# Value products' bank as one room, attention rows joined in DRAM during the recurrence, and softmax inverses two rows at a time

## The chip, the cores and the metric

The kernel runs on one core of a Trainium2 chip. The metric is the device time of one execution in microseconds; several executions give a median. A profile of one further execution tells when each engine worked. The engines are TensorE (matrix products; its weight loads are listed apart), VectorE, ScalarE, GpSimd (POOL in the profile) and SyncE (SP), which here only issues transfers. ScalarE and GpSimd issue transfers as well. 16 DMA engines move the data; transfers issued by SP and ScalarE go over hardware queues (q1, q10), those issued by GpSimd over a software queue (q0).

## What is computed

One step of a one-layer streaming encoder on 1024 prompt positions and 64 sample positions, 1088 columns in all, with 1024 channels:

```python
xn = rms_norm(x, g_pre)
z = xn @ w_in
xa, ga, q, k, v, gb, fl, ma, mb = jnp.split(z, ...)
ua, conv_new = causal_conv(xa, conv_hist, conv_w, conv_b)
ya, h_new = rg_lru(ua, h0, w_rg_a, b_rg_a, w_rg_x, b_rg_x, a_param)      # branch A: recurrence
ya = ya * jax.nn.silu(ga)
logf = jax.nn.log_sigmoid(fl + b_f)
yb = fox_attend(...)             # branch B: softmax(q k^T / 8 + cum_q - cum_k, causal) v, 16 heads of 64
yb = yb.reshape(B, L, W_B) * jax.nn.silu(gb)
u = jnp.einsum('bsnw,nwd->bsnd', jnp.stack([ya, yb], axis=2), w_branch)
gates = jax.nn.sigmoid(jnp.stack([ma, mb], axis=2))
mix = jnp.sum(gates * u, axis=2) @ w_o
h = x + rms_norm(mix, g_post)
ple = jax.nn.sigmoid(h @ w_ple_gate) * (pe @ w_ple_proj)
h = h + rms_norm(ple, g_ple)
```

All is float32. The products reach that precision by splitting each operand into a high part (`xh`, `wh`) and the rest (`xl`, `wl`) and adding three products of parts.

## The kernel before

Data lie with channels on the 128 partitions and positions along the row. The program's stages follow each other on TensorE: the input norm and the value projection; the query and key projections and others in a scheme with sums of weight blocks; attention (about 440 to 850 us); the recurrence of branch A (846 to 1010 us), the branch projections, the merge, the output projection and the embedding part.

**Attention.** A head's 1024 prompt queries are taken in four units of 256. For each unit the scores are made in a bank of the accumulating memory (`s`, L1212 and L1213), VectorE adds the mask and finds the row's minimum (`nm`), ScalarE takes the exponential and the row's sum `sm` (L1191). GpSimd takes the sum to the power of -1 against a column of -1 (`warm`, L1193) and multiplies the row by it (L1194). TensorE turns the row over in 128-column blocks (`tp`, L1244), ScalarE and VectorE split it (`th`, `tl`), and TensorE multiplies by the values (`pv`, L1265 and L1267). The values' high and low parts lie side by side, so the product has 128 partitions: the low half (64 to 127) must be added to the high half (0 to 63). ScalarE copies one half out (`lo`), VectorE adds the other to it (`y`, L1293), and GpSimd stores the 64 x 256 result to `d_y` (L1297). `d_y[k]` holds heads 2k and 2k+1, 128 rows of 1088 columns; the last 64 columns are the sample positions'.

The bank for `pv` is 128 x 2 x 256: two units have a half each, and the planner's list `v_free` has two entries. Eight sample pairs go through the same bank.

**The order of the work** in attention is made by a planner when the program is built. `book(engine, ready, cost, emit)` puts an operation behind what that engine has booked so far; constants give the costs in ns (`A_LO` 380 for the copy, `D_Y` 420 for the add, `G_INV` 220 for the power, `HOP` and `HOP_PE` between engines). Where the next attention step isn't due yet, TensorE gets a step of another projection (`acc`, L179 to L181). In the result each engine's order is fixed, and engines wait for each other by semaphores.

**The recurrence.** Eight blocks of 128 channels. Each brings panels of weights, three to a round of the loop that treats two blocks. A panel of 128 x 1024 weights (512 KB) is loaded by SP into `w_raw` (L265); ScalarE copies it to `wh` and copies the negative of `wh` to `wl` (L90); GpSimd issues an accumulating transfer that adds `w_raw` to `wl` (L297, printed `wl<-w_raw`, from the core's own memory to itself). Only then may `w_raw` be filled with the next panel. The convolved block `u` is split by ScalarE (`uh`, behind the panel's copies in ScalarE's order) and VectorE (`ul`) for the gates' products (`gacc`).

**The branch projection** loads block k of `d_y` and of the gate, `d_gb[k]`, in `branch_in` (L1820 and L1821).

Of the kernel before, what the change touches and what calls it, by code (L numbers as in the profile page):

```python
# [8 lines left out]
F32 = mybir.dt.float32  # L9
F32R = mybir.dt.float32r  # L10
AF = mybir.ActivationFunctionType
ALU = mybir.AluOpType
AX = mybir.AxisListType

P = 128
D = 1024
KT = D // P
SEQ = 1024
DEC = 64
T = SEQ + DEC  # L20
# [3 lines left out]
HD = 64  # L24
# [14 lines left out]
GC = 364  # L39

HOP_PE, HOP = 250.0, 90.0
D_MAX, D_LO, D_Y, D_YS = (240.0, 1.035), (130.0, 1.1), 420.0, 230.0
A_EXP, A_HI, A_LO, A_ST, A_W = (450.0, 0.85), (150.0, 0.88), 380.0, 470.0, 1060.0
G_NORM, G_INV = (260.0, 0.84), 220.0
G_DMA = 860.0
D_W = 1240.0

# [26 lines left out]
def hybrid_step(tc, a, o):  # L74
# [14 lines left out]
    def copy_act(out, in_, scale=1.0):  # L89
        return act.activation(out=out, in_=in_, func=AF.Copy, scale=scale)  # L90
# [8 lines left out]
    d_cq = dram.tile([2, NH, DEC], F32, name="d_cq")  # L99
    d_ma = dram.tile([KT, P, T], F32, name="d_ma")  # L100
    d_mb = dram.tile([KT, P, T], F32, name="d_mb")
    d_y = dram.tile([NP, P, T], F32, name="d_y")
    d_gb = dram.tile([KT, P, T], F32, name="d_gb")
    d_ga = dram.tile([KT, P, T], F32, name="d_ga")
    d_x = [dram.tile([P, T], F32, name=f"d_x{k}") for k in range(2)]
# [107 lines left out]
    def chunk(steps):  # L213
        for _ in range(KT):
            next(steps)
# [325 lines left out]
    at = 0  # L541
# [491 lines left out]
    def spent(ns):  # L1033
        now[0] += ns
# [21 lines left out]
    def per(cost, n):  # L1056
        return cost[0] + cost[1] * n
# [117 lines left out]
        at = book("G", smp_at[p], 490.0, lambda: pool.tensor_copy(vs[:, :, 0, :], v_smp[:, :, :]))  # L1175
        t["vs_at"] = book("G", at, 740.0, lambda: sub(pool, vs[:, :, 1, :], v_smp[:, :, :], f(vs[:, :, 0, :])))

    def tiny2(name):
        return p2.tile([P, 1], F32, name=name, tag=name, bufs=12 if name == "nm" else 8)[:, :]

    def lowest(s, w, out, m, least=-NEG):

# [1 line left out]
        return nm, book("D", now[0] + HOP_PE, per(D_MAX, w), lambda: dve.tensor_tensor_reduce(  # L1184
            out=out, in0=s[:, :w], in1=m, scale=-1.0, scalar=least, op0=ALU.add, op1=ALU.min, accum_out=nm))

    def softmax(at, nm, n, pr):


        sm = tiny2("sm")  # L1190
        at = book("A", at, per(A_EXP, n), lambda: act.activation(  # L1191
            out=pr[:, :n], in_=pr[:, :n], func=AF.Exp, scale=-1.0, bias=nm, accum_out=sm))
        at = book("G", at, G_INV, lambda: pool.tensor_tensor(out=sm, in0=sm, in1=warm[:, :], op=ALU.pow))  # L1193
        return book("G", at, per(G_NORM, n), lambda: pool.tensor_scalar(  # L1194
            out=pr[:, :n], in0=pr[:, :n], scalar1=sm, scalar2=1.0, op0=ALU.mult, op1=ALU.mult))

    def width(q2, par):
        n = 256 * q2 + (par + 1) * P
# [4 lines left out]
    def scores(x, i, pr):  # L1203

        h, q2 = units[x]
        t = heads[h]
        half, par = divmod(i, 2)
        n, w = width(q2, par)
        q0 = (2 * q2 + par) * P
        c = slice(half * w, (half + 1) * w)  # L1210
        s = p2s.tile([P, 512], F32, name="s", tag="s")
        pe.matmul(s[:, :w], t["q1"][:, q0:q0 + P], t["k1"][:, c], start=True, stop=False)  # L1212
        pe.matmul(s[:, :w], t["q2"][:HD + 4, q0:q0 + P], t["k2"][:HD + 4, c], start=False, stop=True)  # L1213
        spent(logits_ns(w))
        nm, at = lowest(s, w, pr[:, c], mask[:, SEQ - n + c.start:SEQ - n + c.stop],
                        nm_first.pop((x, par)) if half else -NEG)
        if c.stop < n:
            nm_first[x, par] = nm
            return at, at
        return at, softmax(at, nm, n, pr)  # L1220

    turned, turned_by = {}, {}
    n_diag = [0]
# [27 lines left out]
        return book("D", at, per(D_LO, n), lambda: sub(dve, tl[:, :n], tp[:, :n], f(th[:, :n])))  # L1251

    pvs = {}
    lo_free = [0.0]
    def values(u, g, h, q2):
        vv = heads_v[h]
        if g == 0:
            pvs[u] = pv_half()
        pv = pvs[u]
        th, tl = turned.pop((u, g))  # L1260
        high = turned_by.pop((u, g))
        def part(j, x, **kw):
            v = vv[:, 2 * g + j, :, :].rearrange("p s d -> p (s d)")
            if g < q2:
                return pe.matmul(pv[:, :256], v, x[:, j * 256:(j + 1) * 256], **kw)  # L1265
            c0 = P if j else 0
            return pe.matmul(pv[:, c0:256], v, x[:, :P] if j else x[:, P:3 * P], **kw)  # L1267

        def high_part(j, stop=False):
            tc.declare_no_dep(part(j, th, start=False, stop=stop).ins, high.ins, reason="ordered through the low part")  # L1270

        if g < q2:
            for j in range(2):
                part(j, tl, start=(g == 0 and j == 0), stop=False)
                high_part(j)
            spent(480.0)
            return
        if q2 == 0:
            part(0, tl, start=True, stop=False)
            part(1, tl, start=False, stop=False)  # L1280
            high_part(1)
        else:
            part(1, tl, start=False, stop=False)
            high_part(1)
            part(0, tl, start=False, stop=False)
        high_part(0, True)
        spent(460.0)
        lo = p2.tile([HD, 256], F32, name="lo", tag="lo", bufs=1)
        y = p2.tile([HD, 256], F32, name="y", tag="y", bufs=3)

        dst = d_y[h // 2][(h % 2) * HD:(h % 2 + 1) * HD, q2 * 256:(q2 + 1) * 256]
        at = book("A", max(now[0] + HOP_PE, lo_free[0]), A_LO, lambda: copy_act(lo[:, :], pv[HD:, :256]))
        at = book("D", at, D_Y, lambda: dve.tensor_tensor(out=y[:, :], in0=pv[:HD, :256], in1=lo[:, :], op=ALU.add))  # L1293
        v_free.popleft()
        v_free.append(at)
        lo_free[0] = at
        book("G", at, G_DMA, lambda: pool.dma_start(dst, y[:, :]))  # L1297


# [10 lines left out]
    def sample_scores(p):  # L1310
        t = smp[p]
        s = p2s.tile([P, 512], F32, name="s", tag="s")
        three(s[:, :LS], *(x[:, :] for x in qs + t["ks"]), True, False)
        pe.matmul(s[:, :LS], cs_q[:, :], cs_k[:, :], start=False, stop=True)
        spent(440.0)
        nm, at = lowest(s, LS, prs_s[:, :LS], mask_s[:, :])
        return at, softmax(at, nm, LS, prs_s)

    def sample_turn(p):
        t = smp[p]  # L1320
# [9 lines left out]
    def sample_values(p):  # L1330
        t = smp.pop(p)
        pv = pv_half()
        for i in range(2):
            pe.matmul(pv[:, :], t["vs"][:, i, 0, :], t["pt"][:, i, :, :].rearrange("p s n -> p (s n)"),
                      start=(i == 0), stop=False)
            pe.matmul(pv[:, :P], t["vs"][:, i, 1, :], t["pt"][:, i, 0, :], start=False, stop=(i == 1))
        spent(458.0)
        ys = p2.tile([P, DEC], F32, name="ys", tag="ys", bufs=1)
        ats = []
        for j in range(2):  # L1340
            js, ks = slice(j * HD, (j + 1) * HD), slice(P + j * HD, P + (j + 1) * HD)
            ats.append(book("A", now[0] + HOP_PE, per(A_HI, HD), lambda js=js, ks=ks: copy_act(ys[js, :], pv[js, ks])))
        for j, at in enumerate(ats):
            js = slice(j * HD, (j + 1) * HD)
            at = book("D", at, D_YS, lambda js=js: dve.tensor_tensor(out=ys[js, :], in0=pv[js, js], in1=ys[js, :],
                                                                     op=ALU.add))
        book("D", at, 0.0, lambda: sp.dma_start(d_y[p][:, SEQ:], ys[:, :]))
        v_free.popleft()
        v_free.append(at)

# [19 lines left out]
    due = {}  # L1372
    s_free = deque([0.0, 0.0, 0.0])
    t_free = deque([0.0, 0.0])
    v_free = deque([0.0, 0.0])
    prs = {}
    seen = {"t": 0, "v": 0}
    last_t = {u: ("t", u, q2) for u, (h, q2) in enumerate(units)}
# [62 lines left out]
            t_free.append(due[step])  # L1441
        done.add(step)

    pool.memset(warm[:, :], -1.0)
    booking = tc.manual_schedule(engines={act.engine, dve.engine, pool.engine})
    booking.__enter__()
    load_head(0)
# [238 lines left out]
    class Held:  # L1686
# [8 lines left out]
        def part(self, ks, evac=None, cs=range(len(CH))):  # L1695
            for c in cs:
# [6 lines left out]
                if evac:  # L1703
                    evac(c, t0, n, self.accs[c][:, :n])

    seq = tc.manual_schedule(engines={act.engine, dve.engine})
    seq.__enter__()
    ga = own_gate(0)
# [4 lines left out]
    for k in range(0, KT - 2, 2):  # L1713
        ga = own_gate(k) if k else ga
        if k == 0:
            run(ga)
        gate(k)
        convolve(k + 1)
        mix_u(k)
        if k:  # L1720
            early_gate(k - 1)
        if k:
            split_y(k - 2)
            chunk(ga)
        split_u(k + 1)
        if k:
            chunk(ga)
            state(k - 1)
            output(k - 1)
            run(ga)  # L1730
        own_gate(k + 1)
        xa = recur_in(k + 2)
        chunk(xa)
        chunk(xa)
        if k:
            split_y(k - 1)
        run(xa)
        gate(k + 1)
        convolve(k + 2)
        mix_u(k + 1)  # L1740
        decay(k)
        xa = recur_in(k + 3)
        split_u(k + 2)
        decay_a(k)
        chunk(xa)
        decay(k + 1)
        decay_a(k + 1)
        chunk(xa)
        root(k)
        root(k + 1)  # L1750
        set_sigmoid()
        state(k)
        output(k)
        run(xa)
# [12 lines left out]
    tag, w = panel()  # L1767
    assert tag == ("f", KT - 1)
    fill = panel_steps(mm, *w, xs, lambda c, t0, n, z: spill(d_mb[KT - 1], t0, n, z))
    chunk(fill)  # L1770
    early_gate(k - 1)
    output(k - 1)
# [44 lines left out]
        return ybpool.tile([P, T], dt, name=name, tag=f"yb{i}{k}")  # L1817

    def branch_in(k, t, z):
        sp.dma_start(t[:, :], d_y[k])  # L1820
        sp.dma_start(z[:, :], d_gb[k])  # L1821
        return t, z

# [574 lines left out]
```

## Time and profile before

| | us |
|---|---|
| runs | 1428.65, 1431.42, 1431.19; median 1431.19 |
| profiled execution, its own time | 1429.49 |
| its span | 1427.5 |
| TensorE busy | 1410.8 |
| VectorE, ScalarE, GpSimd busy | 899.4, 720.5, 436.5 |
| TensorE's granted clock, mean | 0.998 of full |

In a row that groups instructions stand line, engine, operation, what is written and from what, the shape of the output and inputs, the count, then busy time in us and mean ns of one, and then the idle time of the engine just before them with what ended most of it. A row of the waits names the engine and line that waited, whom it waited for, and total, number and longest in us. A row of the timeline has start and duration in us, and in brackets the idle time before. A row of a transfer queue has its packets, the MB and the share of the 16 DMA engines' time in that window. A row of transfers' issues has the count, KB of each and us from issue to landing.

### The profile page before, as it was taken

The numbers are of one execution on the slowest core, as the hardware profiler recorded it, in microseconds if no ns is written. First come the engines' busy times: TensorE is split into PE (matmuls) and PEld (weight loads), VectorE is DVE, ScalarE is ACT, GpSimd is POOL, SyncE is SP. The second block draws the span as 40 slices with busy tenths as digits, with TensorE's granted clock in tenths as the row PEclk, the third lists the DMA queues.
The fourth block names the chain that finished last, engine by engine and source line by source line (L and its number), as shares of the span: only waits on it lengthen the run. The fifth ranks groups of instructions, "written<-read, shape, count | busy, mean of one in ns | idle before, by whom it ended". The sixth has DMA issues, their size and how long they took to land.

```text
span 1427.5 us, 25022 instructions
## 1 busy us (share of the span) xinstructions
PE 1410.8 (99%) x9217; PEld 1358.0 (95%) x9217; DVE 899.4 (63%) x1638; ACT 720.5 (50%) x1339; POOL 436.5 (31%) x652
## 2 busy tenths in 40 slices
PE   9999999999999999999999999999999999999997
PEld 8999999999999999999999999999999999888887
DVE  5564766564432666666666656898767474777654
ACT  5423544442222666666666657777544232565443
POOL 0012322233204777768776841221011000000001
PEclk9999999999999999999999999999999999999999
DMA  6667556765247764556566545564467774224211
GB/s 225 214 133 107 150 155 193 162 180 141 85 122 194 182 130 131 137 110 151 123 150 131 84 101 106 83 101 84 165 211 264 252 237 136 113 74 150 78 48 45
DMA packets 138919, 201.20 MB, mean 141 GB/s; under 512 B 24372, under 2 KB 98844, under 8 KB 137772
## 3 DMA queue, kind: packets, MB, share of 16 engines
q1 hardware_dynamic: 119436, 158.96, 44.2%
q0 software_dynamic: 8160, 23.25, 5.9%
q10 hardware_dynamic: 11200, 17.38, 3.4%
q8 instruction: 73, 1.20, 0.3%
q14 instruction: 50, 0.41, 0.1%
HBM read 131.60 MB, written 66.36 MB: 139 GB/s over the span
## 4 chain that ended last, share of the span: by engine, by line
PE 82%; DVE 6%; DMA 5%; ACT 3%; issue 3%; POOL 1%; SPq 0%; DVEq 0%; ACTq 0%; POOLq 0%
PE quad L844 17%; PE acc L179 11%; PE acc L181 11%; PE acc L180 11%; PE q L2042 5%; PE tp L1244 4%; PE pv L1265 3%; PE s L1213 2%; PE s L1212 2%; PE pv L1267 2%; PE vacc L179 1%; PE vacc L180 1%; PE vacc L181 1%; DMA w_raw<-in_w_in 1%; PE vacc L500 1%
## 5 line engine op out<-in xcount | busy, mean ns | idle before, releaser
L179 PE MATMUL acc<-xh,wh 128*128 128x364 f32 x720 | 237.6, 330 | 0.2 <-ACT st L90 0.2
L181 PE MATMUL acc<-xh,wl 128*128 128x364 f32 x720 | 235.8, 328 | 0.0
L180 PE MATMUL acc<-xl,wh 128*128 128x364 f32 x720 | 235.8, 327 | 0.0
L179 PEld LDWEIGHTS acc<-xh,wh 128*128 128x128 f32 x720 | 135.4, 188 | 1.2 <-ACT st L90 0.5
L180 PEld LDWEIGHTS acc<-xl,wh 128*128 128x128 f32 x720 | 135.3, 188 | 0.8
L181 PEld LDWEIGHTS acc<-xh,wl 128*128 128x128 f32 x720 | 135.1, 188 | 0.0
L90 ACT ACTIVATE wh<-w_raw 128x1024 fp32r<-128x1024 f32 (+1 forms) x66 | 63.4, 962 | 86.4 <-PE quad L844 34.4
L93 DVE TENSOR_TENSOR wl<-w_raw,wh 128x1024 fp32r<-128x1024 f32 (+1 forms) x55 | 62.5, 1138 | 67.6 <-ACT wh L90 47.0
L1193 POOL TENSOR_TENSOR sm<-sm,warm 128x1 f32<-128x1 f32 x136 | 79.2, 582 | 57.0 <-ACT pb L1191 21.8
L93 DVE TENSOR_TENSOR tl<-tp,th 128x512 fp32r<-128x512 f32 x96 | 65.6, 687 | 38.7 <-ACT th L90 37.9
L844 PE MATMUL quad<-xh,wh 128*128 128x272 f32 x416 | 87.4, 291 | 1.8 <-ACT p__3330 L90 1.8
L844 PE MATMUL quad<-xl,wh 128*128 128x272 f32 x416 | 86.1, 288 | 0.0
L844 PE MATMUL quad<-xh,wl 128*128 128x272 f32 x416 | 86.0, 288 | 0.0
L1191 ACT ACTIVATE pb<-pb,nm 128x896 f32<-128x896 f32 (+1 forms) x64 | 63.3, 989 | 24.0 <-DVE nm L1184 21.3
L90 ACT ACTIVATE th<-tp 128x512 fp32r<-128x512 f32 x96 | 56.4, 592 | 31.0 <-PE tp L1244 30.3
L2338 POOL TENSOR_TENSOR junk<-ple,g_ple 128x256 f32<-128x256 f32 x4 | 3.8, 956 | 213.2 <-DVE ple L2295 213.2
L1212 PE MATMUL s<-k,q 128*128 128x128 f32 (+2 forms) x192 | 67.5, 353 | 0.0
L844 PEld LDWEIGHTS quad<-xh,wh 128*128 128x128 f32 x416 | 65.3, 188 | 2.3 <-ACT p__3330 L90 2.0
L1213 PE MATMUL s<-k,q 68*128 68x128 f32 (+2 forms) x192 | 65.3, 344 | 0.5 <-issue 0.5
L844 PEld LDWEIGHTS quad<-xh,wl 128*128 128x128 f32 x416 | 65.5, 188 | 0.0
L844 PEld LDWEIGHTS quad<-xl,wh 128*128 128x128 f32 x416 | 65.4, 188 | 0.0
L1194 POOL TENSOR_SCALAR pb<-pb,sm 128x896 f32<-128x896 f32 (+1 forms) x64 | 61.5, 962 | 6.2
(744 smaller groups left out, 4230.4 us busy)
## 6 DMA issues: line engine op xcount, KB each, us to landing
w_raw<-in_w_in SPq DMA_DIRECT2D x56, 256.0 KB
q<-d_q SPq DMA_DIRECT2D x48, 256.0 KB
k<-d_k SPq DMA_DIRECT2D x48, 256.0 KB
w_raw<-in_w_in SPq DMA_DIRECT2D x64, 128.0 KB
w_raw<-in_w_branch SPq DMA_DIRECT2D x32, 256.0 KB
wl<-w_raw POOLq DMA_DIRECT2D x11, 512.0 KB, 4.5
wraw<-in_w_in SPq DMA_DIRECT2D x20, 256.0 KB
d_k<-oh ACTq DMA_DIRECT2D x16, 272.0 KB
```

The lines of the kernel that those rows point to most:

```text
L90: return act.activation(out=out, in_=in_, func=AF.Copy, scale=scale)
L93: return eng.tensor_tensor(out=out, in0=in0, in1=in1, op=ALU.subtract)
L179: pe.matmul(out, ah, bh, start=start, stop=False)
L180: pe.matmul(out, ah, bl, start=False, stop=False)
L181: pe.matmul(out, al, bh, start=False, stop=stop)
L844: pe.matmul(acc[:, c, :CW], l[:, k, :], r[:, k, c * CW:(c + 1) * CW], start=(first and k == 0 and p == 0), stop=(k == 3 and p == 2), skip_ ...
L1191: at = book("A", at, per(A_EXP, n), lambda: act.activation(out=pr[:, :n], in_=pr[:, :n], func=AF.Exp, scale=-1.0, bias=nm, accum_out=sm))
L1193: at = book("G", at, G_INV, lambda: pool.tensor_tensor(out=sm, in0=sm, in1=warm[:, :], op=ALU.pow))
L1194: return book("G", at, per(G_NORM, n), lambda: pool.tensor_scalar(out=pr[:, :n], in0=pr[:, :n], scalar1=sm, scalar2=1.0, op0=ALU.mult, op1 ...
L1212: pe.matmul(s[:, :w], t["q1"][:, q0:q0 + P], t["k1"][:, c], start=True, stop=False)
L1213: pe.matmul(s[:, :w], t["q2"][:HD + 4, q0:q0 + P], t["k2"][:HD + 4, c], start=False, stop=True)
L2042: pe.matmul(acc, l[:, k, :], r[:, k, :], start=(first and k == 0 and i == 0), stop=(k == 3 and i == 2), skip_group_check=not first)
```

## The change

- `d_y` becomes `[8, 2, 128, 1024]`: for each head both halves of the product are stored, and the sample's 64 columns go to a tile of their own, `d_ys`.
- A unit's bank is emptied by one ScalarE copy of 128 x 256 to `y`; GpSimd stores it whole. `v_free` has one entry. For a sample pair there is the same copy, and VectorE adds its halves from there.
- `join_rows(k)` adds, in DRAM, the low halves of block k's two heads to the high halves: one accumulating transfer on GpSimd's queue. Two stand in each round of the recurrence's loop, two behind the recurrence's last panel.
- `branch_in` reads block k in two loads of 64 rows and one of the sample's columns.
- The sums of a unit's two blocks of queries stand in one tile of two columns; VectorE takes both reciprocals in one operation. The planner's cost for it is `INV` 165; the column `warm` is no longer filled for it.

```diff
-    def softmax(at, nm, n, pr):
...
-        at = book("G", at, G_INV, lambda: pool.tensor_tensor(out=sm, in0=sm, in1=warm[:, :], op=ALU.pow))
+    def inverse(at, sm, k):
+        return book("D", at, INV, lambda: dve.reciprocal(out=sm[:, :k], in_=sm[:, :k]))
...
+        if par == 0:
+            sm = tiny2("sm", 2)
+            sums[x] = sm, powers(at, nm, n, pr, sm[:, :1]), pr, n
+            return at, at
+        sm, first, pr0, n0 = sums.pop(x)
+        done_ = inverse(max(first, powers(at, nm, n, pr, sm[:, 1:])), sm, 2)
+        return at, normal(normal(done_, n0, pr0, sm[:, :1]), n, pr, sm[:, 1:])
...
-        lo = p2.tile([HD, 256], F32, name="lo", tag="lo", bufs=1)
-        y = p2.tile([HD, 256], F32, name="y", tag="y", bufs=3)
-        dst = d_y[h // 2][(h % 2) * HD:(h % 2 + 1) * HD, q2 * 256:(q2 + 1) * 256]
-        at = book("A", max(now[0] + HOP_PE, lo_free[0]), A_LO, lambda: copy_act(lo[:, :], pv[HD:, :256]))
-        at = book("D", at, D_Y, lambda: dve.tensor_tensor(out=y[:, :], in0=pv[:HD, :256], in1=lo[:, :], op=ALU.add))
+        y = p2.tile([P, 256], F32, name="y", tag="y", bufs=3)
+        dst = d_y[h // 2, h % 2][:, q2 * 256:(q2 + 1) * 256]
+        at = book("A", now[0] + HOP_PE, A_Y, lambda: copy_act(y[:, :], pv[:, :256]))
         v_free.popleft()
         v_free.append(at)
...
-    v_free = deque([0.0, 0.0])
+    v_free = deque([0.0])
...
+    def join_rows(k):
+        tc.keep_in_program_order(pool.dma_start(d_y[k][:, :HD, :], d_y[k][:, HD:, :],
+                                 accum_op=ALU.add, max_dma_last_dim=4096))
...
         own_gate(k + 1)
         xa = recur_in(k + 2)
+        join_rows(k)
...
         xa = recur_in(k + 3)
+        join_rows(k + 1)
...
     fill = panel_steps(mm, *w, xs, lambda c, t0, n, z: spill(d_mb[KT - 1], t0, n, z))
+    join_rows(k)
+    join_rows(k + 1)
...
     def branch_in(k, t, z):
-        sp.dma_start(t[:, :], d_y[k])
+        for j in range(2):
+            sp.dma_start(t[j * HD:(j + 1) * HD, :SEQ], d_y[k, j][:HD, :])
+        sp.dma_start(t[:, SEQ:], d_ys[k])
         sp.dma_start(z[:, :], d_gb[k])
```

GpSimd's order in the first round of the recurrence, before (`wl<-w_raw` is the panel's transfer, `fin`, `xp` and `st` are small tiles of the convolution and the gates):

```order
L297 DMA wl<-w_raw 128x1024
L1569 COPY fin<-xp 128x3
L1570 COPY fin<-xp 128x3
L1545 MEMSET xp 128x3
L1546 MEMSET xp 128x1
L1548 COPY xp<-vt 128x3
L1537 MEMSET st 128x256
L297 DMA wl<-w_raw 128x1024
```

and the same place with the change:

```order
L298 DMA wl<-w_raw 128x1024
L1711 DMA d_y<-d_y 2x64x1024
L1573 COPY fin<-xp 128x3
L1574 COPY fin<-xp 128x3
L298 DMA wl<-w_raw 128x1024
L1549 MEMSET xp 128x3
L1550 MEMSET xp 128x1
L1552 COPY xp<-vt 128x3
L1711 DMA d_y<-d_y 2x64x1024
```

A join (`d_y<-d_y`) now stands behind one panel's transfer and ahead of the next one's, and a second join three operations behind that one.

VectorE's order at the end of two units of attention, before (`tl`, `diag…l` are low parts of turned rows, `nm` a row's minimum):

```order
L93 TENSOR_TENSOR tl<-tp_5864,th 128x512
L93 TENSOR_TENSOR diag0l<-tp_5884,diag0h 128x384
L1293 TENSOR_TENSOR y<-pv,lo 64x256
L93 TENSOR_TENSOR tl<-tp_5931,th 128x512
L93 TENSOR_TENSOR tl<-tp_5947,th 128x512
L1293 TENSOR_TENSOR y<-pv,lo 64x256
```

With the change no row of VectorE reads `pv`; ScalarE's order around the copies is

```order
L90 ACTIVATE th<-tp_5898 128x512
L90 ACTIVATE y<-pv 128x256
L90 ACTIVATE diag1h<-tp_5915 128x384
L90 ACTIVATE st<-acc 128x364
L90 ACTIVATE ksh<-tps 128x128
L90 ACTIVATE diag2h<-tp_5949 128x384
L90 ACTIVATE y<-pv 128x256
```

where `y<-pv` of 128 partitions stands in the place of `lo<-pv` of 64, and nothing else of the engine follows it for the same unit.

More of the change, by code (lines that the diff above doesn't have):

```diff
@@ L41 @@
 HOP_PE, HOP = 250.0, 90.0
-D_MAX, D_LO, D_Y, D_YS = (240.0, 1.035), (130.0, 1.1), 420.0, 230.0
-A_EXP, A_HI, A_LO, A_ST, A_W = (450.0, 0.85), (150.0, 0.88), 380.0, 470.0, 1060.0
-G_NORM, G_INV = (260.0, 0.84), 220.0
+D_MAX, INV, D_LO, D_YS = (240.0, 1.035), 165.0, (130.0, 1.1), 230.0
+A_EXP, A_HI, A_Y, A_ST, A_W = (450.0, 0.85), (150.0, 0.88), 380.0, 470.0, 1060.0
+G_NORM = (260.0, 0.84)
 G_DMA = 860.0
@@ L101, in hybrid_step @@
     d_mb = dram.tile([KT, P, T], F32, name="d_mb")
-    d_y = dram.tile([NP, P, T], F32, name="d_y")
+    d_y = dram.tile([NP, 2, P, SEQ], F32, name="d_y")
+    d_ys = dram.tile([NP, P, DEC], F32, name="d_ys")
     d_gb = dram.tile([KT, P, T], F32, name="d_gb")
@@ L1176, in load_sample, with tiny2 @@
         t["vs_at"] = book("G", at, 740.0, lambda: sub(pool, vs[:, :, 1, :], v_smp[:, :, :], f(vs[:, :, 0, :])))
-    def tiny2(name):
-        return p2.tile([P, 1], F32, name=name, tag=name, bufs=12 if name == "nm" else 8)[:, :]
+    def tiny2(name, n=1):
+        return p2.tile([P, n], F32, name=name, tag=name, bufs=12 if name == "nm" else 8)[:, :]
     def lowest(s, w, out, m, least=-NEG):
@@ L1185, in lowest, with powers, normal @@
             out=out, in0=s[:, :w], in1=m, scale=-1.0, scalar=least, op0=ALU.add, op1=ALU.min, accum_out=nm))
-    def softmax(at, nm, n, pr):
-        sm = tiny2("sm")
-        at = book("A", at, per(A_EXP, n), lambda: act.activation(
+    def powers(at, nm, n, pr, sm):
+        return book("A", at, per(A_EXP, n), lambda: act.activation(
             out=pr[:, :n], in_=pr[:, :n], func=AF.Exp, scale=-1.0, bias=nm, accum_out=sm))
-        at = book("G", at, G_INV, lambda: pool.tensor_tensor(out=sm, in0=sm, in1=warm[:, :], op=ALU.pow))
+    def inverse(at, sm, k):
+        return book("D", at, INV, lambda: dve.reciprocal(out=sm[:, :k], in_=sm[:, :k]))
+    def normal(at, n, pr, sm):
         return book("G", at, per(G_NORM, n), lambda: pool.tensor_scalar(
             out=pr[:, :n], in0=pr[:, :n], scalar1=sm, scalar2=1.0, op0=ALU.mult, op1=ALU.mult))
+    sums = {}
     def width(q2, par):
@@ L1219, in scores @@
             return at, at
-        return at, softmax(at, nm, n, pr)
+        if par == 0:
[5 more added lines that the diff above has]
+        return at, normal(normal(done_, n0, pr0, sm[:, :1]), n, pr, sm[:, 1:])
     turned, turned_by = {}, {}
@@ L1253, in hybrid_step @@
     pvs = {}
-    lo_free = [0.0]
     def values(u, g, h, q2):
@@ L1287, in values @@
         spent(460.0)
-        lo = p2.tile([HD, 256], F32, name="lo", tag="lo", bufs=1)
-        y = p2.tile([HD, 256], F32, name="y", tag="y", bufs=3)
-        dst = d_y[h // 2][(h % 2) * HD:(h % 2 + 1) * HD, q2 * 256:(q2 + 1) * 256]
-        at = book("A", max(now[0] + HOP_PE, lo_free[0]), A_LO, lambda: copy_act(lo[:, :], pv[HD:, :256]))
-        at = book("D", at, D_Y, lambda: dve.tensor_tensor(out=y[:, :], in0=pv[:HD, :256], in1=lo[:, :], op=ALU.add))
+        y = p2.tile([P, 256], F32, name="y", tag="y", bufs=3)
+        dst = d_y[h // 2, h % 2][:, q2 * 256:(q2 + 1) * 256]
+        at = book("A", now[0] + HOP_PE, A_Y, lambda: copy_act(y[:, :], pv[:, :256]))
         v_free.popleft()
         v_free.append(at)
-        lo_free[0] = at
         book("G", at, G_DMA, lambda: pool.dma_start(dst, y[:, :]))
@@ L1316, in sample_scores @@
         nm, at = lowest(s, LS, prs_s[:, :LS], mask_s[:, :])
-        return at, softmax(at, nm, LS, prs_s)
+        sm = tiny2("sm", 2)[:, :1]
+        return at, normal(inverse(powers(at, nm, LS, prs_s, sm), sm, 1), LS, prs_s, sm)
     def sample_turn(p):
@@ L1337, in sample_values @@
         spent(458.0)
+        yv = p2.tile([P, 256], F32, name="y", tag="y", bufs=3)
         ys = p2.tile([P, DEC], F32, name="ys", tag="ys", bufs=1)
-        ats = []
+        at = book("A", now[0] + HOP_PE, A_Y, lambda: copy_act(yv[:, :], pv[:, :256]))
+        v_free.popleft()
+        v_free.append(at)
         for j in range(2):
             js, ks = slice(j * HD, (j + 1) * HD), slice(P + j * HD, P + (j + 1) * HD)
[L1342 to L1349, printed above, removed]
+            at = book("D", at, D_YS, lambda js=js, ks=ks: dve.tensor_tensor(
+                out=ys[js, :], in0=yv[js, js], in1=yv[js, ks], op=ALU.add))
+        book("D", at, 0.0, lambda: sp.dma_start(d_ys[p], ys[:, :]))
     units = [(h, q2) for h in range(NH) for q2 in (0, 3, 1, 2)]
@@ L1442, in go @@
         done.add(step)
-    pool.memset(warm[:, :], -1.0)
     booking = tc.manual_schedule(engines={act.engine, dve.engine, pool.engine})
@@ L1704, in part @@
                     evac(c, t0, n, self.accs[c][:, :n])
+    def join_rows(k):
+        tc.keep_in_program_order(pool.dma_start(d_y[k][:, :HD, :], d_y[k][:, HD:, :], accum_op=ALU.add, max_dma_last_dim=4096))
     seq = tc.manual_schedule(engines={act.engine, dve.engine})
```

## The prediction

> **What bounds the kernel now.** The first look is the page: busy time by engine, then the windows of the two stages that the change touches, attention (440 to 852 us) and the recurrence (846 to 1000 us; columns: busy us of PE, PEld, DVE, ACT, POOL).
>
> ```profile
> PE 1410.8 (99%) x9217; PEld 1358.0 (95%) x9217; DVE 899.4 (63%) x1638; ACT 720.5 (50%) x1339; POOL 436.5 (31%) x652
> 440.00:852.00 412.00, 409.91 (x2833) 399.03 (x2833) 254.20 (x674) 259.38 (x593) 285.01 (x469) 1.00 0.59 135
> 860.00:900.00 40.00, 40.00 (x244) 40.00 (x243) 29.17 (x29) 32.28 (x48) 8.23 (x19) 1.00 0.52 80
> 900.00:950.00 50.00, 50.00 (x303) 50.00 (x302) 43.92 (x46) 34.25 (x51) 10.64 (x23) 1.00 0.60 91
> 950.00:1000.00 50.00, 49.83 (x301) 49.52 (x300) 45.29 (x46) 37.42 (x57) 10.35 (x17) 1.00 0.47 90
> ```
>
> TensorE bounds both. Work taken from other engines buys nothing by itself; only a TensorE wait that goes, or a new one, moves the end. So the second look is at what TensorE waits for in attention: total us, times, longest.
>
> ```profile
> PEld pv L1265 <- DVE y L1293: 2.1, 4, 0.7
> PEld pv L1267 <- DVE y L1293: 1.4, 4, 0.4
> PEld pv L1267 <- ACT lo L90: 0.2, 1, 0.2
> PEld pv L1265 <- DVE ys L1345: 0.2, 1, 0.2
> ```
>
> Matmul ends are modelled, so the weight loads are the better witness: 3.9 us of waiting belong to the value products' bank, in ten waits. The timeline shows one:
>
> ```profile
> 504.63 0.38 ACT L90 ACTIVATE lo<-pv 64x256 f32<-64x256 f32 x1
> 505.91 0.28 PE L1265 MATMUL pv<-th,vv 128*128 128x256 f32 x1
> 506.29 0.42 DVE L1293 TENSOR_TENSOR y<-pv,lo 64x256 f32<-64x256 f32 x1 [1.95 <-ACT st L90]
> 506.75 0.19 PEld L1267 LDWEIGHTS pv<-diag0l,vv 128*128 128x128 f32 x1 [0.36 <-DVE y L1293]
> ```
>
> The copy `lo` of a unit is done at 505.01, but its add `y` starts only at 506.29, just after the *next* unit's products in the bank's other half ended (506.19); then the products behind it wait until the add is through. Two rooms in one bank are no two independent rooms.
>
> **The bank and the sums.** These rows price what attention loses and gains:
>
> ```profile
> L1193 POOL TENSOR_TENSOR sm<-sm,warm 128x1 f32<-128x1 f32 x136 | 79.2, 582 | 57.0 <-ACT pb L1191 21.8 <-DVE diag2l L93 8.1 <-DVE diag0l L93 7.6
> L1293 DVE TENSOR_TENSOR y<-pv,lo 64x256 f32<-64x256 f32 x64 | 26.4, 412 | 32.9 <-ACT lo L90 11.9 <-PE pv L1265 7.8 <-ACT st L90 3.9
> L90 ACT ACTIVATE lo<-pv 64x256 f32<-64x256 f32 x64 | 24.4, 382 | 20.4 <-PE pv L1265 9.4 <-PE pv L1267 7.9 <-PE pv L1336 1.2
> L155 DVE RECIPROCAL r_y<-r_y x18: 154/164/165, 5.9 to 1421.8; 128x1 f32<-128x1 f32 x16, 64x1 f32<-64x1 f32 x2
> ```
>
> GpSimd loses 136 powers, 79.2 us. VectorE loses 64 adds, 26.4 us, and gains 72 reciprocals (64 of two rows, 8 of one): 72 x 0.164 = 11.8 us. ScalarE's copy keeps its 256 columns and takes in 128 partitions instead of 64; the partitions work side by side, so I leave it at 0.38. The row store doubles to 128 KB, 64 times. All this lies under TensorE (VectorE is busy 254 of 412 us, ScalarE 259, GpSimd 285) and counts nothing. Were the cover gone, the added reciprocals would cost at most their own 11.8.
>
> On TensorE's path the add is gone and one copy frees the bank: the 3.9 us can go whole. Against it: there is one room now, so the next unit's first product waits for that copy, and where it stands behind a softmax exponential (about 1 us) TensorE stands too. The same copy in the same place cost 0.2 us, once, in the kernel before. So the bounds are 0 and -3.9; I take **-3.4**, nearer the full gain for that 0.2.
>
> **The joins.** What the add did is now done by eight accumulating DRAM-to-DRAM transfers on GpSimd's queue, with access pattern 2 x 64 x 1024: 128 rows of 4 KB. Six stand two to a loop, directly or a few small operations behind a panel's `wl` transfer, two behind the last one. The nearest thing in the trace is that `wl` transfer, also accumulating, 128 rows of 4 KB (window 868 to 876 us):
>
> ```profile
> q0 software_dynamic: 144, 0.52, 34.7%
> wl<-w_raw POOLq DMA_DIRECT2D x1, 512.0 KB, 4.6
> ```
>
> 144 packets are 128 rows and 16 markers; 8 us x 16 engines x 0.347 = 44.4 engine-us, or **0.347 us a row**. Eight rows on each of 16 engines make 2.8 us; 64 rows on each of two make **22.2 us**. Which one holds is the main question, since `wl` has 128 as its outer count and a join has 2. The hardware queue answers by count (window 491 to 501.5 us):
>
> ```profile
> q1 hardware_dynamic: 496, 1.61, 66.1%
> q<-d_q SPq DMA_DIRECT2D x3, 256.0 KB
> k<-d_k SPq DMA_DIRECT2D x3, 256.0 KB
> k<-d_rows SPq DMA_DIRECT2D x1, 16.0 KB
> q<-d_rows SPq DMA_DIRECT2D x1, 16.0 KB
> ```
>
> Six loads of 64 rows and two of 4 rows are 392 rows. With a marker for each engine used, 6 x 16 + 2 x 4 = 104 markers, and 496 packets come out exactly; spread over 16, the small ones would give 520. A transfer thus goes to as many engines as its outermost count allows. By that a join, outermost count 2, goes to two. No transfer on GpSimd's own queue in this trace has a small outer count, so this is carried over from the other queue.
>
> The Trainium skill ("DMA: Bandwidth & Descriptors", "Why a DMA increments its semaphore by 16 and not by 1") says that the number of engines is the largest one up to 16 that divides the slowest dimension of both access patterns, on either kind of queue: the 496 packets agree for the hardware queue, and no run here shows the software queue. It also names an exception in which the software queue spreads some direct copies over all 16; by that the first rival below holds.
>
> **What waits behind a join.** The chain of waits shows a panel's round (start, us, what), with `wl`'s next issue on GpSimd, TensorE's gates, and its first use of that panel, of the one after, and of one a loop later:
>
> ```profile
> 868.79 4.57 DMA wl<-w_raw
> 873.42 0.37 SPq L265
> 874.86 5.52 DMA w_raw<-in_w_in
> 881.39 1.05 ACT wh L90
> 884.56 1.29 DVE ul L93
> 883.82 0.85 POOL L297 DMA_DIRECT2D wl<-w_raw  x1 [3.62 <-ACT wl L90]
> 888.72 0.33 PE L180 MATMUL gacc<-ul,g_h 128*128 128x364 f32 x1
> 891.57 0.33 PE L179 MATMUL acc<-xh,wh 128*128 128x364 f32 x1
> 903.47 0.33 PE L179 MATMUL acc<-xh,wh 128*128 128x364 f32 x1
> 933.31 0.33 PE L179 MATMUL acc<-xh,wh 128*128 128x364 f32 x1
> ```
>
> `wl` lands at 873.36; only then may `w_raw` be refilled (landed 880.38); ScalarE splits it; the next `wl` is issued at 883.82 and lands about 888.4; TensorE uses it at 891.57, 3.2 us later. The loop of three panels takes 933.31 - 891.57 = 41.7 us of a fully busy TensorE, and a panel's own round is some 13.3 us where nothing holds it, so there is hardly a microsecond a panel to spare.
>
> With a join of 22.2 us on two engines behind `wl`, the next `wl` has 8 of its rows on each of those engines behind it: 22.2 + 2.8 = 25 us from landing to landing. First loop: 873.4 + 2 x 25 = 923.4, needed at 903.47: 19.9 late. Each of the next two loops: 25 + 25 + 13.3 = 63.3 against 41.7, 21.6 late. Sum 63.1. A plain 4 KB row is cheaper: the window of 496 packets gives 10.5 x 16 x 0.661 / 392 = 0.283 us. At that price a join is 18.1 us, the round 20.9, and the sum 11.7 + 2 x 13.4 = **+38**, the low bound. The high bound is that `w_raw`'s rows on the hardware queue are held on those engines too. The trace shows such a hold, in the window 851.3 to 853.9 us, while a `wl` transfer ran:
>
> ```profile
> 851.33 1.86 SPq L1542 DMA_DIRECT2D st<-in_w_rg_a  x2
> q0 software_dynamic: 128, 0.52, 106.9%
> ```
>
> Loads issued from 851.33 on moved no packet (that queue has no row in the answer) until the accumulating rows were done. If that holds for 64 rows, the round is 22.2 + 2.3 (the load's 8 x 0.283) + 3.4 (880.38 to 883.82) + 4.6 = 32.5. First loop 873.4 + 65 - 903.5 = 34.9, later ones 32.5 x 2 + 13.3 - 41.7 = 36.6 each, sum **+108**. The hold is seen over four or five rows only, so between the ends I take the middle, **+73**.
>
> The Trainium skill (same page, "Queues, rings and completion order") has an engine drain a packet of some 9 to 17 descriptors before it turns to another queue; the hold of the `st` loads agrees, and it stands between both ends.
>
> Later, `branch_in` issues three loads of the attention rows for one, on SP:
>
> ```profile
> 1017.81 0.43 SPq L1820 DMA_DIRECT2D in_h<-d_y  x1
> ```
>
> That is 8 x 2 x 0.43 = 6.9 us more of SP, spread over some 100 us in which SP waits for free rooms most of the time; behind these issues stand the weights of the next panel. Twice three issues ahead of a weight load that TensorE awaits would be 2.6 us. I take 0, bounds 0 and +3.
>
> **The sum**, against the profiled execution (span 1427.5, its own time 1429.5): 1429.5 - 3.4 + 73 = 1499.1. The median of the runs, 1431.2, lies 1.7 above: **1501 us**. Own range of this case: 1429.5 - 3.9 + 38 = 1464 to 1429.5 + 108 + 3 = 1540.
>
> **Rivals.** *The joins spread over all 16 engines* (not slower). For it: `wl`'s 144 packets hold 16 markers, so the one software transfer looked at is spread so. Against it: the count of the 496. Each join is 2.8 us; a refill of `w_raw` waits 0 to 2.8 us, and the gates' slack behind `ul` (885.85 to 888.72) takes that up. 1431.2 - 3.4 + 0 to 2 = 1428 to 1430, point **1428**.
>
> *The wait changes its name only.* `pv` now waits for `y` on ScalarE, since one room allows no product ahead of the copy; with joins hidden, bounds -3.9 + 1 and +16 (one copy in four, 16, behind an exponential of 1 us). For it: ScalarE's copy sat idle before 20.4 us, waiting for `pv`, so it is prompt most times but not always. Point **1431**. That the bank isn't freed earlier, so the change does not do what it says, is this case.
>
> **How the numbers follow.** Two engines: 0.60, all slower. Spread: 0.27, of which 0.17 beyond the 0.2% (2.9 us) that a measurement can tell, 0.10 within. Renamed wait: 0.13, of which 0.02 faster, 0.08 same, 0.03 slower. So faster 0.19, same 0.18, slower 0.63. The range takes in both rivals and leaves out the topmost joins: 1426 to 1535.
>
> **What would show it.** Right: a join lands 20 us or more after issue; in 870 to 1000 us TensorE idles, waiting for `wl` and `ul`; `w_raw` loads double; no `pv <- y` of VectorE is left. Wrong: joins land in 4 to 6 us, with TensorE full in those windows (spread); `pv` waits on ScalarE's `y` (renamed).

## The result, and the profile after

The changed kernel takes 1491.0 us (median, 1490.0 to 1491.5) against 1430.7 of the kernel before on the same chip: 1.0423 times as long, 95% interval 1.0405 to 1.0441. One execution of a run below, the inverses row by row, took 2811.9 us, far off the pace of the other four, and no median here counts it. The profiled execution's span is 1488.9 us against 1427.5, 61.4 longer.

Where the 61.4 us lie is read from three groups of TensorE's products: the last of the query and key projections (`quad`), the gates of the recurrence (`gacc`), the first branch products (`held`). In each row "a to b" is the start of the group's first and last instruction. Before:

```profile
L844 PE MATMUL quad<-t4h,wh x104: 285/288/398, 160.4 to 432.7; 128*128 128x272 f32 x104
L179 PE MATMUL gacc<-uh,g_h x48: 323/327/333, 858.7 to 993.5; 128*128 128x364 f32 x48
L179 PE MATMUL held<-yah,wh x48: 320/328/432, 1014.3 to 1050.2; 128*128 128x364 f32 x32, 128*128 128x360 f32 x16
```

and after:

```profile
L845 PE MATMUL quad<-t4h,wh x104: 285/288/392, 160.5 to 433.3; 128*128 128x272 f32 x104
L180 PE MATMUL gacc<-uh,g_h x48: 323/328/674, 855.0 to 1050.7; 128*128 128x364 f32 x48
L180 PE MATMUL held<-yah,wh x48: 322/328/337, 1071.2 to 1111.7; 128*128 128x364 f32 x32, 128*128 128x360 f32 x16
```

- Attention, from the end of `quad` to the first `gacc`: 426.0 before, 421.7 after, **-4.3 us**. (The expectations count from the very last `quad` product, half a microsecond later: 425.5 and 421.2.)
- The recurrence, first to last `gacc`: 134.8 before, 195.7 after, **+60.9 us**.
- The first branch products: 35.9 before, 40.5 after, **+4.6 us**.
- Together +61.2. The rest of the program, before `quad` and after `held`, is as long as it was within 0.6 us.

What TensorE waits for in the recurrence (window 850 to 1070 us, the weight loads' waits):

```profile
PEld acc L182 <- DMA wl<-w_raw: 31.8, 3, 11.5
PEld gacc L180 <- ACT uh L90: 16.7, 2, 11.6
PEld gacc L181 <- DVE ul L93: 2.1, 2, 1.0
```

Before, the recurrence had no such wait. The three add up to 50.6 us of the 60.9. The rest is clock. The recurrence's 816 weight loads were busy for 135.1 us before and for 145.4 after, 10.3 us more. After one of these waits, of 10.5 us for `wl`, TensorE worked at half its rate for some 5 us, as the third number from the end shows, the granted clock (window 979 to 984, the wait ends at 979.6; then 985 to 996):

```profile
979.00:984.00 5.00, 4.39 (x14) 4.39 (x15) 2.35 (x4) 2.12 (x2) 3.51 (x8) 0.50 0.42 132
985.00:996.00 11.00, 11.00 (x68) 11.00 (x67) 2.90 (x3) 4.23 (x9) 0.55 (x3) 1.00 0.63 92
```

Behind the waits stand late transfers. Shown are the join's own row (issue's duration min/median/max in ns, first and last start; then us to landing), the median of `wl` on the page, and, from the chain of waits (start, us), two refills of `w_raw` and two `wl` transfers:

```profile
L1711 POOL DMA_DIRECT2D d_y<-d_y x8: 1404/1772/2628, 868.9 to 1047.4; - x8
DMA to landing us min/median/max: 25.2/27.0/30.5
wl<-w_raw POOLq DMA_DIRECT2D x11, 512.0 KB, 6.4
873.29 24.65 DMA w_raw<-in_w_in
924.16 22.57 DMA w_raw<-in_w_in
962.12 17.44 DMA wl<-w_raw
1025.52 17.54 DMA wl<-w_raw
```

A join lands after 27 us, a refill takes 23 to 25 where it took 5.5, and the panel's transfer behind a second join 17.5 where it took 4.5. The loop's period shows in the issues of `wl` three panels apart:

```profile
917.65 0.86 POOL L298 DMA_DIRECT2D wl<-w_raw  x1
982.31 0.87 POOL L298 DMA_DIRECT2D wl<-w_raw  x1 [0.88 <-ACT wl L90]
1045.84 0.87 POOL L298 DMA_DIRECT2D wl<-w_raw  x1 [4.29 <-ACT wl L90]
```

64.7 and 63.5 us, against 41.7 before.

How a join holds a refill can be seen where both are nearly alone (window 966 to 978 us):

```profile
q0 software_dynamic: 87, 0.29, 12.3%
q1 hardware_dynamic: 72, 0.03, 1.5%
```

0.29 MB are 71 rows of 4 KB (the join's, and from about 976.6 on the panel's, which stand behind them), and 12.3% of 16 engines is two engines. The hardware queue moved nearly as many in that time: 68 of its 72 packets are rows of 512 bytes, which are those of `w_raw` (each of its four transfers has 256 of them, 16 an engine). The two queues' rows go in turn: in each of 19 steps of 0.35 us from 966.35 to 973.0 stand two rows of the join and two of the hardware queue (three once), so one of each for each engine. A pair takes 12 us x 2 engines / 71 = 0.338 us. An engine that a join uses has 64 join rows and 64 refill rows to move: 64 pairs take 21.6 us, and both end together.

The pages count the engines a second way. The software queue's packets of the whole program, as changed, then with the joins turned and without joins (both runs below):

```profile
q0 software_dynamic: 17504, 31.69, 8.0%
q0 software_dynamic: 10336, 31.64, 8.3%
q0 software_dynamic: 9184, 27.44, 6.5%
```

Against the run without joins a turned join has (10336 - 9184) / 8 = 144 packets, its 128 rows and 16 markers. A join as the change makes it has 1040, which is 16 x 65: with 128 rows and, as before, 16 markers, 896 = 14 x 64 small packets are left (926 of the 930 in the window 871.0 to 872.8, ahead of the first join's rows, are under 512 bytes). So it looks as if each of the 14 engines that have no row gets one small packet for every row that the other two have.

### The profile page after: what moved, and what is told of

Same layout as the page of the kernel before. It is cut to its first block, busy times and chain, and to the rows that moved or that the text cites. A ratio compares the mean times of both kernels' runs of the same rounds, so it can differ in the third digit from the quotient of the medians.

```text
span 1488.9 us, 24933 instructions
## 1 busy us (share of the span) xinstructions
PE 1421.3 (95%) x9217; PEld 1369.0 (92%) x9217; DVE 888.3 (60%) x1646; ACT 713.5 (48%) x1331; POOL 364.6 (24%) x523
## 4 chain that ended last, share of the span: by engine, by line
PE 79%; DMA 12%; issue 3%; DVE 2%; ACT 2%; SPq 1%; POOL 0%; ACTq 0%; DVEq 0%; POOLq 0%
PE quad L845 16%; PE acc L182 11%; PE acc L180 11%; PE acc L181 11%; DMA w_raw<-in_w_in 6%; PE q L2055 5%; PE tp L1255 4%; PE pv L1275 3%; PE s L1218 2%; DMA wl<-w_raw 2%; PE s L1217 2%; PE pv L1277 2%; PE vacc L180 1%; PE vacc L181 1%; PE vacc L182 1%
## 5 line engine op out<-in xcount | busy, mean ns | idle before, releaser
L182 PE MATMUL acc<-xh,wl 128*128 128x364 f32 x720 | 238.9, 332 | 30.9 <-DMA wl<-w_raw 30.9
L180 PE MATMUL acc<-xh,wh 128*128 128x364 f32 x720 | 242.4, 337 | 0.0
L182 PEld LDWEIGHTS acc<-xh,wl 128*128 128x128 f32 x720 | 137.4, 191 | 31.8 <-DMA wl<-w_raw 31.8
L90 ACT ACTIVATE wh<-w_raw 128x1024 fp32r<-128x1024 f32 (+1 forms) x66 | 63.5, 963 | 137.9 <-DMA w_raw<-in_w_in 46.3
L1190 ACT ACTIVATE pb<-pb,nm 128x896 f32<-128x896 f32 (+1 forms) x64 | 63.3, 988 | 20.5 <-DVE nm L1185 19.9
L845 PEld LDWEIGHTS quad<-xh,wl 128*128 128x128 f32 x416 | 65.5, 188 | 0.0
L181 PE MATMUL acc<-ybl,wh 128*128 128x364 f32 (+1 forms) x192 | 62.9, 328 | 0.0
L1255 PE MATMUL tp<-ident,pb 128*128 128x128 f32 x416 | 62.9, 272 | 0.0
```

The costliest lines, as they stand in the source:

```text
L180: pe.matmul(out, ah, bh, start=start, stop=False)
L181: pe.matmul(out, ah, bl, start=False, stop=False)
L182: pe.matmul(out, al, bh, start=False, stop=stop)
L845: pe.matmul(acc[:, c, :CW], l[:, k, :], r[:, k, c * CW:(c + 1) * CW], start=(first and k == 0 and p == 0), stop=(k == 3 and p == 2), skip_ ...
L1190: return book("A", at, per(A_EXP, n), lambda: act.activation(out=pr[:, :n], in_=pr[:, :n], func=AF.Exp, scale=-1.0, bias=nm, accum_out=sm))
L1255: pe.transpose(tp[:, i * P:(i + 1) * P], pr[par][:, kb * P:(kb + 1) * P], ident[:, :])
```

## The experiments

All are compared with the kernel before on the same chip (medians 1429.2 to 1429.8 us there).

**The access pattern turned round.**

```diff
-        tc.keep_in_program_order(pool.dma_start(d_y[k][:, :HD, :], d_y[k][:, HD:, :], accum_op=ALU.add, max_dma_last_dim=4096))
+        lo, hi = (d_y[k][:, j * HD:(j + 1) * HD, :].rearrange("j p s -> p j s") for j in (1, 0))
+        tc.keep_in_program_order(pool.dma_start(hi, lo, accum_op=ALU.add, max_dma_last_dim=4096))
```

> The changed kernel with one thing different: the two dimensions of each join's access pattern are swapped, 64 x 2 x 1024 instead of 2 x 64 x 1024. Same bytes, same 128 rows of 4 KB, same eight transfers at the same places. Theory (the outermost count sets the number of engines, and two engines of 64 rows hold up the panels): a join lands in 4 to 7 us instead of 25 to 30, the waits of the products for wl (30.9 us) and of the gates for uh (16.1 us) are gone, and only the shorter attention is left, 1431 - 4 = 1427 us, bounds 1424 to 1432. Rival (adding from DRAM to DRAM is slow by itself): landing stays above 20 us and the time near 1491. Rival (the time goes to GpSimd, which issues a join in 1.4 to 2.6 us ahead of wl): the time stays above 1450 although joins land early.

1427.95 us, 0.9985 times the kernel before (0.9976 to 0.9994). The join's landing and TensorE's waits in the window 840 to 1150 us:

```profile
L1712 POOL DMA_DIRECT2D d_y<-d_y x8: 928/1322/1355, 868.9 to 995.1; - x8
DMA to landing us min/median/max: 7.5/8.0/8.5
PEld held L180 <- DVE st_a L1878: 1.6, 1, 1.6
PEld held L180 <- DVE sg_e L1675: 0.6, 1, 0.6
PEld acc L180 <- ACT st L90: 0.4, 1, 0.4
```

and the software queue while the first join moves (window 873 to 875 us, 93 of its 128 rows):

```profile
q0 software_dynamic: 93, 0.38, 102.7%
```

That is all 16 engines, against two above. The same bytes in the same rows at the same places cost some 63 us less with 64 as the outermost count. So the number of engines is the cause; adding in DRAM is not slow by itself, and GpSimd still spends 1.3 us on each issue without harm. The landing was a little above the 4 to 7 us expected.

**No joins.**

```diff
     def join_rows(k):
-        tc.keep_in_program_order(pool.dma_start(d_y[k][:, :HD, :], ...))
+        pass
```

> The changed kernel without the eight joins: the low halves are never added, so that part of the attention result is left out. All else stands. Theory: the whole loss of 60 us hangs on the joins, so 1427 us (1424 to 1431), the attention's gain of 4 alone, equal to the run with swapped dimensions within 3 us. Rival (the new bank, the doubled stores or the split loads in the branch projection cost too): above 1435.

1424.25 us, ratio 0.9959 (0.9947 to 0.9972). The whole loss hangs on the joins. Beside this run the turned joins still cost 3.7 us, slightly more than expected; the run with the last two joins moved forward, below, shows where.

**Shorter rows on two engines.**

```diff
-... accum_op=ALU.add, max_dma_last_dim=4096))
+... accum_op=ALU.add, max_dma_last_dim=1024))
```

> The changed kernel with the joins cut into rows of 1 KB, still outermost 2: 256 rows on each of two engines. Theory (an engine takes rows of the two queues in turn, one by one): w_raw's 64 rows of 512 bytes per engine each wait for one short row (estimated 0.347 / 4 = 0.087 us) instead of one of 0.33, so the refill lands in some 64 x (0.04 + 0.09) = 8 us instead of 24, while a join still takes 22 us or more and the next wl still queues behind it: 1445 to 1475 us. Rival (an engine holds a whole join before it turns to the other queue): the refill still lands with the join, after more than 20 us, and the time stays at 1480 to 1500.

1503.5 us, ratio 1.052 (1.0507 to 1.0534): slower still, and the time missed both forecasts (1445 to 1475 and 1480 to 1500). Its page shows that one half of the theory held and the other half met something new: the weight loads' waits, the join's group with the idle time before its issue, and its landing.

```profile
PEld acc L182 <- DMA wl<-w_raw: 63.6, 5, 19.2
PEld acc L182 <- DVE wl L93: 3.6, 1, 3.6
L1711 POOL DMA_DIRECT2D d_y<-d_y x8 | 24.4, 3045 | 67.8 <-issue 67.8
DMA to landing us min/median/max: 28.6/30.6/42.2
898.14 3.01 POOL L1711 DMA_DIRECT2D d_y<-d_y  x1 [15.61 <-issue]
902.23 1.05 POOL L298 DMA_DIRECT2D wl<-w_raw  x1
```

The gates' wait for `uh`, 16.7 us in the changed kernel, is gone: a refill that takes turns with short rows is early enough. The first one's 0.52 MB, issued from 872.1 on, went by between 873 and 882 us, beside the first join. But GpSimd stands 67.8 us ahead of its joins with nothing that the profile names to wait for; the second join is issued at 898.1, after 15.6 us, with the next `wl` behind it at 902.2, 22 us behind the one before. In this run the first join had moved its last row at about 897. So a join of 512 short rows seems to fill the queue, and GpSimd cannot issue the next one until rows have left it. That reading is an inference from the times; it wasn't tested by itself. The count of packets fits: (42080 - 9184) / 8 = 4112 a join here, 16 x 257, four times those of the change. The rival, an engine that holds a whole join before it turns to the other queue, falls, since under it the refills would have stayed late.

**All joins at the end.**

```diff
         xa = recur_in(k + 2)
-        join_rows(k)
...
         xa = recur_in(k + 3)
-        join_rows(k + 1)
...
-    join_rows(k)
-    join_rows(k + 1)
+    for j in range(KT):
+        join_rows(j)
```

> The changed kernel with all eight joins issued one behind the other after the recurrence's last panel; none in the loop. Theory (each join takes two engines, and the next one the next two): eight joins fill all 16 engines, all have landed after some 30 us, and only one panel's load is held: 1427 + 10 to 25 = 1437 to 1452 us. Rival (all joins go to the same two engines): the last one lands after 8 x 22 = 178 us and the branch projection waits for it, above 1530. Rival (the cost goes with the joins' bytes, wherever they stand): near 1490.

1452.7 us, ratio 1.0159 (1.0146 to 1.0172), 0.7 us above the theory's range.

```profile
L1711 POOL DMA_DIRECT2D d_y<-d_y x8 | 11.8, 2529 | 20.0 <-issue 20.0
DMA to landing us min/median/max: 26.9/37.4/44.4
PEld held L180 <- ACT wh L90: 20.3, 2, 15.8
```

Eight joins of about 22 us on one pair of engines would have needed 178 us; the slowest landed after 44.4, later than the 30 expected. So successive joins go to different engines. Against the run without joins the same bytes cost 28 us here and 67 in the loop. So the bytes alone do not set the cost; that it goes by how often a panel meets a join is the reading that fits. Again GpSimd stood, 20.0 us, between issues.

**The inverses alone, row by row, and as in the change.** The first edit puts the kernel before's inverses on VectorE one at a time; the second takes over the change's functions, two rows in one reciprocal. Both keep two rooms and VectorE's adds.

```diff
-        at = book("G", at, G_INV, lambda: pool.tensor_tensor(out=sm, in0=sm, in1=warm[:, :], op=ALU.pow))
+        at = book("D", at, 165.0, lambda: dve.reciprocal(out=sm, in_=sm))
```

> The kernel before with one edit of the change alone: the inverse of a softmax sum by VectorE's reciprocal (one row at a time, 136 of about 0.16 us) instead of GpSimd's power (136 of 0.58 us). Bank, store and rows as before. Theory (the gain of attention, 425.5 to 421.3 us from the last quad product to the first gate product, is the freed bank): nothing gained, 1428 to 1432 us, and the waits of pv for VectorE's y stay or grow. Rival (the gain is the shorter way from sum to inverse): 1425 to 1428, that stretch 422 us or less.

```diff
-    def softmax(at, nm, n, pr):
...
+    def powers(at, nm, n, pr, sm):
...
+    def inverse(at, sm, k):
...
+    def normal(at, n, pr, sm):
...
```

> The kernel before with the change's inverses exactly (two rows' sums in one tile, one VectorE reciprocal for both); two rooms, VectorE's add and the stores as before, no joins. Theory (the freed bank alone gains, and the inverses on VectorE cost where a bank's adds are on VectorE too): the ten waits of pv stay, last quad product to first gate product 425 us or more, 1429 to 1440 us. Rival (only the reciprocals one row at a time were bad, paired ones gain): 422 us or less, below 1428.

Row by row: 1440.8 us, ratio 1.008 (1.0066 to 1.0093). That is outside the theory's 1428 to 1432 and on the far side from the rival. In the profiled execution (1441.8 us) attention takes 438.2 us (433.0 to 871.2), 12.2 more than before. A wait of 4.5 us for a softmax row on GpSimd is part of that, beside those that were there (window 435 to 850 us):

```profile
PEld tp L1244 <- POOL pb L1194: 4.5, 1, 4.5
PEld pv L1265 <- DVE y L1293: 2.0, 4, 0.7
```

The planner made another order out of the other costs, in which the last value product started at 857.1 instead of 844.7; what in it makes up the rest of the 12.2 us stays open. In pairs: 1429.5 us, ratio 1.0002 (0.9993 to 1.0010), attention 426.0 as before. Its waits:

```profile
PEld pv L1275 <- DVE y L1303: 2.3, 7, 0.5
PEld pv L1277 <- DVE y L1303: 1.0, 1, 1.0
PEld pv L1275 <- DVE ys L1356: 0.9, 2, 0.5
```

The inverses as the change makes them gain nothing, and `pv` waits for VectorE's `y` and `ys` as before, 4.2 us in all.

**One room, with the inverses back on GpSimd.** The kernel with turned joins, and

```diff
-        return book("D", at, INV, lambda: dve.reciprocal(out=sm[:, :k], in_=sm[:, :k]))
+    pool.memset(warm[:, :], -1.0)
...
+        for i in range(k):
+            at = book("G", at, 220.0, lambda i=i: pool.tensor_tensor(out=sm[:, i:i + 1], in0=sm[:, i:i + 1],
+                                                                     in1=warm[:, :], op=ALU.pow))
+        return at
```

> The run with swapped dimensions, with the inverses back on GpSimd, by a power for each row as in the kernel before. One room and one copy stay. Theory (freed bank): the stretch from the last quad product to the first gate product stays near 421.5 us and the time within 1.5 us of the run with swapped dimensions, 1427 to 1430. Rival (inverse): the stretch goes back to 425 us and the time to 1431 or more.

1426.8 us, ratio 0.9981 (0.9973 to 0.9990), attention 421.7 us. With the run in pairs above this settles the inverses: the gain of 4.3 us comes with the one room and the single copy that empties it, none of it with the inverses. Whether two rooms emptied by such a copy would gain as much was not tried.

**The last two joins moved forward.** The kernel with turned joins, and

```diff
+        if k:
+            join_rows(KT - 3 + k // 2)
...
-    join_rows(k)
-    join_rows(k + 1)
     chunk(fill)
```

> The run with swapped dimensions, with the last two joins moved forward from behind the recurrence's last panel, where the load of the branch weights starts, to the second and third round of the loop, one each behind the panel that has no join. Theory (what is left of the joins' cost are the 1.8 us that the first branch products run longer than before, 38.0 against 36.2 us, behind the late branch weights and gates): these go, 1 to 3 us less than the run with swapped dimensions, 1425 to 1427. Rival (three joins in a round are too many): the recurrence's 135 us from first to last gate product grow, 1428 or more.

1424.86 us, ratio 0.9968 (0.9956 to 0.9981): 0.3% less than the kernel before. The first branch products take 35.9 us again, as before the change (they took 37.7 with the turned joins alone), and the recurrence's 134.7 us did not grow:

```profile
L180 PE MATMUL gacc<-uh,g_h x48: 323/327/333, 854.4 to 989.1; 128*128 128x364 f32 x48
L180 PE MATMUL held<-yah,wh x48: 320/328/430, 1010.0 to 1045.9; 128*128 128x364 f32 x32, 128*128 128x360 f32 x16
DMA to landing us min/median/max: 7.4/7.8/7.9
```

The time is within 0.6 us of the run without joins, so there they are all but hidden.

> The run with swapped dimensions and the last two joins moved forward, with the inverses back on GpSimd, one power a row. Theory (inverses count nothing once the bank is one room): within 1.5 us of the run with the reciprocals, 1424 to 1426. Rival (GpSimd's power was 1 us better in the earlier pair of runs for a reason): 1423 or less. Rival (the reciprocals are worth something): 1427 or more.

With the inverses on GpSimd as well (the two edits above together): 1424.6 us, ratio 0.9968 (0.9956 to 0.9980). With one room the inverses count nothing either way.

**Half the rows on two engines at a time.**

```diff
+        for j in range(2):
+            hi, lo = (d_y[k][j, i * HD:(i + 1) * HD, :].rearrange("p (c s) -> c p s", c=2) for i in range(2))
+            tc.keep_in_program_order(pool.dma_start(hi, lo, accum_op=ALU.add, max_dma_last_dim=4096))
```

> The changed kernel with each join as two transfers, one per head, of 2 x 64 x 512: outermost 2 again, 64 rows of 2 KB on each of two engines, the second transfer on the next two. Theory (time of a join = rows per engine x time of a row; refill and join rows in turn): a row of 2 KB takes about 0.18 us (between 0.10 for 1 KB and 0.33 for 4 KB), so a join lands 12 to 17 us after issue, a refill of w_raw takes about 64 x (0.18 + 0.04) = 14 us, and the time lies between the two ends, 1432 to 1460. Rival (the number of transfers with two engines counts, not their rows): as the change, 1480 to 1500, or more.

1460.5 us, ratio 1.0215 (1.0199 to 1.0230), half a microsecond above the theory's range.

```profile
DMA to landing us min/median/max: 15.8/17.5/21.4
PEld acc L182 <- DMA wl<-w_raw: 10.9, 5, 2.5
PEld gacc L180 <- ACT uh L90: 10.1, 2, 5.1
```

The same outermost count with rows half as long gives landings of 17.5 instead of 27.0 us and half the loss: the waits for `wl` go from 31.8 to 10.9 us, those for `uh` from 16.7 to 10.1. More transfers with two engines each are not what costs; the length of time that an engine's rows last is.

## Why the prediction was right, point by point

The forecast of 1501 us, by joins on two engines, is the case that came. Of the sum's terms:

- *The bank, -3.4.* Right, slightly small: -4.3 us, a little beyond the bound of -3.9. All waits of `pv` are gone. The bound counted only the waits at the weight load; the kernel with pairs and two rooms still takes 426.0, and the runs with one room take 421.6 to 422.3, so the whole difference belongs to the room and its copy. The fear of a copy behind an exponential didn't come true: no `pv` waits for ScalarE's `y`.
- *The joins on two engines, from the hardware queue's count of 496 packets.* Right: 12.3% of 16 engines in the window above, 1040 packets a join instead of 144, and 8.0 instead of 27.0 us when the outermost count is turned. The Trainium skill ("DMA: Bandwidth & Descriptors", "Why a DMA increments its semaphore by 16 and not by 1") states this for both kinds of queue; the two landings agree for the software queue, and the exception that spreads a direct copy over 16 did not apply to these.
- *The price of a row, 0.347 us from the `wl` transfer.* Right: 0.338 us for a join's row and the refill's row that goes in between, as counted above.
- *+73 as the middle of +38 and +108.* Measured: +60.9 in the recurrence and +4.6 at the first branch products, 65.5. The size was near, partly by luck: 73 was the middle of two bounds, and neither describes what ran; the sum without a hold, 63.1, was nearer. Two of its steps were wrong and two terms were missing. First, the rounds were laid out as if a refill served the next panel. `w_raw` has two halves that take turns (`raw_half` in the code), and a refill serves the panel after next; so refills and `wl` transfers are late on different panels, and the loop's period came to 64, near the 63.3 of the sum without a hold, for another reason. Second, the "hold" read from the late `st` loads. Rows of the two queues take turns; the refill is as late as it is because it has 64 small rows for a join's 64 large ones. The run with 1 KB rows agrees: no hold, and the gates' wait gone. Of the 2.6 us in which the `st` loads of before moved nothing, 1.2 are what such loads took with the queue free (issued at 865.97 and 880.22, first packets at 867.2 and 881.4); why the other 1.4 were lost was not tried. The Trainium skill (same page, "Queues, rings and completion order") has an engine drain a packet of several descriptors before it turns; here the records show one row for one, two and two in steps of 0.35 us, and the measurement decides. The terms that were missing: about 10 us of the 60.9 are the halved clock after the waits; and the last two joins hold the load of the branch weights, the +4.6 at the first branch products (35.9 us again without joins, or with these two moved forward).
- *The smaller edits at 0.* Right within what can be told: without joins the kernel is 5.5 us faster than before, no less than attention gained, and the first branch products take 35.9 us there in spite of the three loads for one.
- *The rivals.* The spread over 16 engines did not happen, but its price (1428) is what the turned joins give, 1427.95. What spoke for it, the 16 markers of `wl`, does not tell: a join on two engines brings packets for all 16 as well, 1040 = 16 x 65. The renamed wait did not happen either.
- *The ends of the range.* 1491 lies inside the case's own range of 1464 to 1540.

## What to carry to other kernels

Look at the outermost count of a transfer's access pattern before its size: with 2 there, 512 KB lasted 27 us and made every transfer that shared those two engines late, with 64 there it lasted 8 and cost 3.7 us in all, or 0.6 with the last two moved. A transfer that nobody waits for can still set the pace of a loop through the rows it puts in front of others, so look for a place where no load is due that something waits for. And two rooms in one bank, emptied by a copy and an add, were worth 4.3 us less here than one room that a single short copy empties; which of the two differences counts was not separated.

## What the runs showed of the hardware that was not expected

- Rows of the software and the hardware queue went through an engine in turn, one to one: 4 KB rows beside 512-byte rows, 0.338 us a pair. A load in small rows suffers by it: a refill of 64 such rows an engine took 5.5 us before and 23 to 25 beside a join.
- Successive joins with two engines each used different engines: eight issued one behind the other landed after 27 to 44 us, not 178.
- A join on two engines brought 896 small packets besides its 128 rows, with 1 KB rows 3584 besides 512; on 16 engines it brought none. That they lie on the other 14 engines is inferred from the counts, and what they cost was not tried.
- GpSimd stood 67.8 us ahead of joins of 512 rows each, and 20.0 us in a series of eight joins of 128 rows, with no semaphore to wait for; in the changed kernel 0.9 us.
- The granted clock was 0.50 over 5 us behind a wait of 10.5 us, so that a wait cost more than its own length.
